# Keeping the written order in the feed-forward blocks of a two-layer trunk, and adding the residual inside PSUM

## The chip, the cores and the metric

The kernel runs on one core of one Trainium2 chip. The core has four engines that matter here: TensorE (PE in the profile; its weight loads are listed apart as PEld), VectorE (DVE), ScalarE (ACT) and GpSimd (POOL). A fifth, SyncE (SP), issues almost all transfers. The metric is the time on the device in microseconds, as the median of the runs shown. All arithmetic is meant to agree with a float32 reference.

## The reference, cut to what matters

Two layers; each has a token mixer (a gated recurrence with cross-attention into 256 memory tokens beside it) and a feed-forward part. The change lies in the feed-forward part:

```python
SEQ, D_MODEL, D_FF = 256, 2048, 5632
hn = _rmsnorm(h, norm_ffn[layer])
gate, up = jnp.split(hn @ w_gate_up[layer], 2, axis=-1)      # w_gate_up: 2048 x 11264
h = h + (jax.nn.silu(gate) * up) @ w_down[layer]             # w_down: 5632 x 2048
```

## The kernel before, in words

**Products.** The kernel multiplies float32 numbers by splitting each into a high part, rounded to the type fp32r, and a low part that holds the rest. A product is then three matmuls: high by high, high by low, low by high (L333, L334, L335 in the gate and up products; L249, L250, L251 in the down products). The tokens' factor is split once; the weights are split as they come. A weight tile is loaded in float32 into a buffer `raw` of 128 x 4 x 512 numbers (four of these buffers), by `new_raw`. `split` then lets ScalarE write the high part (a CAST, L207) and VectorE the low one (a subtraction, L208) into a tile `parts`, of which there are six; a tile holds two rows of 512. So each weight passes through SP's queue, ScalarE, VectorE and TensorE in turn.

**The feed-forward part.** The 5632 hidden columns are handled in eleven blocks of 512, b0 to b10 (`ffn`, `up_block`). A block takes the 2048 rows of the weights in eight pairs of 128 rows, and computes for the two halves of the tokens both gate and up: per pair a 2 x 2 by 2 x 2 product of tiles. `project_halves` does this in one of three ways, by the letter of the pair in the table `KINDS`. Letter S (Strassen's scheme, in Winograd's form) takes seven products, 21 matmuls; its sums of weight tiles are three more operations on VectorE (L350 on 1024 columns, L351 and L352 on 512), and the tiles are split in four pieces named `parts<number>a` to `d`: a of 512 columns, b, c, d of 1024. Letter O takes eight products, 24 matmuls, without sums, in pieces a and b. Letter H also takes eight products and 24 matmuls, with one sum of 512 columns and a third piece of 512. The seven partial results of the block, p1 to p7, lie in seven of the eight PSUM banks. From block 3 on, all blocks have the letters SSOSSOSS.

After the last pair of a block the seven results are added up into `s` and `e` (one COPY on ScalarE, L830; seven additions on VectorE, L833), the gate goes through SiLU (L835, ScalarE) and is multiplied by up (L836, VectorE). The product `s` is transposed on TensorE and split again (`make_quad`, L148 and L149), as the tokens' factor of the down product.

**The down products.** The down product sums over the eleven blocks in six parts (`PARTS`: block 0; blocks 1 and 2; 3 and 4; ... 9 and 10), each for four column groups of 512: `down(i, n)`. Two of these are done after each of the blocks b1 to b10, and the four of the last part at the end. A down product of two blocks is 48 matmuls in two banks, and `add_h` (L414, VectorE) then adds each bank of 128 x 512 to the residual `h`, which stays in SBUF.

**What sets the order.** The instructions are written in this order, but the framework's scheduler decides which goes first on each engine, within what buffers and data allow. Pieces of work such as the transposes are handed to a list (`later`) and let out between steps (`step`).

## Time and profile before

| what | value |
|---|---|
| median of 3 runs | 2323.36 us (2322.37 to 2323.85) |
| the profiled execution's own time | 2322.12 us |
| its span on the core | 2320.3 us |
| mean granted TensorE clock | 0.998 |
| matmul instructions (PE) | 11034, busy 2297.6 us (99% of the span) |
| weight loads (PEld) | 11034, busy 1934.7 us (83%) |
| VectorE | 2262 instructions, busy 1887.7 us (81%) |
| ScalarE | 1643 instructions, busy 1261.2 us (54%) |
| bytes moved by transfers | 435.51 MB, mean 188 GB/s |

The span is from the first to the last record on the core; the execution's own time is 1.8 us longer. A PE matmul's record lasts longer than the distance to the next one, because matmuls are pipelined; so PE is called busy nearly throughout, also where it waits for short times, and its waits are better read from the starts of its rows. By the starts of its instructions the span falls into: the memory tokens' product (5 to 105 us), the first mixer (105 to 447) with its output product (447 to 541), the first feed-forward part (541 to 1250), the second mixer with its output product (1250 to 1610), and the second feed-forward part (1610 to 2320). In the first feed-forward part block 8 begins at 1008.57 us, block 9 at 1071.72 and block 10 at 1134.89.

In the views, "f_p" are the gate and up results, "fd" the down results, "hf" the tokens' factor of the gate and up products, "s_8" the gated product of a block and its split halves, "tp_" a transposed tile in PSUM, "parts" the split weights. Single pieces keep their numbers: parts172 to parts179 are the eight pairs of block 8, and parts184 to parts191 those of block 9 in the first layer. The names are shared between the kernel before and the kernel after.

### The profile page before, as it was taken

The page shows a single profiled execution, that of the slowest core. Times are in us where ns is not written, and L with a number is a line of the kernel's source. Part 1 is how long each engine was busy: PE and PEld are TensorE (multiplying, and loading weights), DVE is VectorE, ACT ScalarE, POOL GpSimd, SP SyncE. Part 2 cuts the span into 40 slices and gives each one's busy share as a digit, 9 for nine tenths or more (in the row PEclk, how much of TensorE's full clock was granted, in tenths as well). Part 3 has the DMA queues.
Part 4 walks back from the last instruction along what each step waited for, and adds up shares of the span by engine and source line. Part 5 has one row for each costly group of instructions (what it writes and reads, how often), then busy time and mean ns, then how long its engine had stood idle before and what let it go on. Part 6 is the DMA issues. An engine that isn't in the chain of part 4 may idle for free.

```text
span 2320.3 us, 28901 instructions
## 1 busy us (share of the span) xinstructions
PE 2297.6 (99%) x11034; PEld 1934.7 (83%) x11034; DVE 1887.7 (81%) x2262; ACT 1261.2 (54%) x1643; POOL 22.2 (1%) x39
## 2 busy tenths in 40 slices
PE   9999999999999999999999999999999999999998
PEld 7888888888887888888889999988887888888886
DVE  5566565668999999999985665567999999999995
ACT  7543534455555555555555654455555555555563
POOL 0000000000000000000000000000000000000000
PEclk9999999999999999999999999999999999999999
DMA  8554545455556556566565445555555556656563
GB/s 316 192 172 162 164 150 176 145 182 176 186 188 212 200 188 205 189 209 208 183 226 167 150 150 167 161 199 164 178 203 198 201 187 210 202 189 210 200 217 127
DMA packets 229211, 435.51 MB, mean 188 GB/s; under 512 B 10028, under 2 KB 38992, under 8 KB 228816
## 3 DMA queue, kind: packets, MB, share of 16 engines
q1 hardware_dynamic: 227776, 429.40, 55.5%
q10 hardware_dynamic: 1296, 4.26, 0.5%
q8 instruction: 86, 1.41, 0.2%
q14 instruction: 53, 0.43, 0.1%
HBM read 430.48 MB, written 3.15 MB: 187 GB/s over the span
## 4 chain that ended last, share of the span: by engine, by line
PE 63%; DVE 25%; issue 6%; ACT 4%; DMA 0%; ACTq 0%; DVEq 0%; POOLq 0%; SPq 0%
PE f_p L334 5%; PE f_p L335 5%; PE f_p L333 4%; DVE raw L350 4%; DVE parts L208 4%; PE fd L250 3%; PE fd L249 3%; PE fd L251 3%; PE wo L251 3%; PE wo L249 3%; PE wo L250 3%; DVE raw L351 2%; DVE raw L352 2%; PE hgate L249 1%; PE gv L249 1%
## 5 line engine op out<-in xcount | busy, mean ns | idle before, releaser
L208 DVE TENSOR_TENSOR parts<-raw,parts 128x1024 fp32r<-128x1024 f32 (+3 forms) x490 | 557.7, 1147 | 289.1 <-ACT parts L207 288.2
L207 ACT CAST parts<-raw 128x1024 fp32r<-128x1024 f32 (+3 forms) x490 | 476.8, 991 | 424.6 <-PE wo L251 64.4
L350 DVE TENSOR_TENSOR raw<-raw 128x1024 f32<-128x1024 f32 x118 | 143.6, 1217 | 0.2
L351 DVE TENSOR_TENSOR raw<-raw 128x512 f32<-128x512 f32 x118 | 81.6, 692 | 3.9
L352 DVE TENSOR_TENSOR raw<-raw 128x512 f32<-128x512 f32 x118 | 81.6, 692 | 3.8
L414 DVE TENSOR_TENSOR h<-fd,h 128x512 f32<-128x512 f32 x94 | 61.9, 684 | 6.2 <-PE fd L251 6.1
L833 DVE TENSOR_TENSOR e<-f_p,e 128x512 f32<-128x512 f32 x66 | 44.9, 680 | 0.0
L835 ACT ACTIVATE s<-s,rf_r 128x512 f32<-128x512 f32 x44 | 31.8, 722 | 6.9 <-DVE s L833 6.9
L836 DVE SCALAR_TENSOR_TENSOR s<-e,rf_r,s 128x512 f32<-128x512 f32 x44 | 32.3, 742 | 0.0
L562 DVE COPY_PREDICATED sch<-mask,slh 96x512 f32<-96x512 uint8 (+3 forms) x15 | 10.8, 721 | 25.1 <-PE slh L578 25.1
L833 DVE TENSOR_TENSOR s<-f_p,e 128x512 f32<-128x512 f32 x44 | 29.5, 682 | 0.0
L578 PEld LDWEIGHTS slh<-Q,K 128*96 128x96 f32 (+3 forms) x240 | 25.4, 176 | 1.4
L249 PE MATMUL wo<-parts,y_3h 128*128 128x512 f32 x64 | 25.9, 405 | 0.0
L249 PE MATMUL wo<-parts,y_0h 128*128 128x512 f32 x64 | 25.7, 402 | 0.0
L250 PE MATMUL fd<-parts,s_3h 128*128 128x512 f32 x64 | 25.4, 396 | 0.0
L249 PE MATMUL fd<-parts,s_0h 128*128 128x512 f32 x64 | 25.3, 396 | 0.0
L249 PE MATMUL fd<-parts,s_2h 128*128 128x512 f32 x64 | 25.3, 396 | 0.0
L249 PE MATMUL fd<-parts,s_6h 128*128 128x512 f32 x64 | 25.3, 396 | 0.0
L249 PE MATMUL fd<-parts,s_4h 128*128 128x512 f32 x64 | 25.3, 396 | 0.0
L250 PE MATMUL fd<-parts,s_5h 128*128 128x512 f32 x64 | 25.3, 396 | 0.0
L249 PE MATMUL fd<-parts,s_8h 128*128 128x512 f32 x64 | 25.3, 396 | 0.0
L250 PE MATMUL fd<-parts,s_0h 128*128 128x512 f32 x64 | 25.3, 396 | 0.0
(5486 smaller groups left out, 7396.4 us busy)
## 6 DMA issues: line engine op xcount, KB each, us to landing
raw<-in_w_gate_up_dram SPq DMA_DIRECT2D x352, 512.0 KB, 4.0
raw<-in_w_down_dram SPq DMA_DIRECT2D x88, 1024.0 KB, 5.0
raw<-in_hgrn_w_in_dram SPq DMA_DIRECT2D x52, 1024.0 KB, 5.0
raw<-in_gla_w_in_dram SPq DMA_DIRECT2D x48, 768.0 KB, 4.3
raw<-in_w_out_dram SPq DMA_DIRECT2D x32, 1024.0 KB, 4.9
raw<-in_w_mem_kv_dram SPq DMA_DIRECT2D x15, 1024.0 KB, 8.2
raw<-in_gla_w_in_dram SPq DMA_DIRECT2D x8, 528.0 KB, 3.7
mtok<-in_mem_dram SPq DMA_DIRECT2D x4, 512.0 KB
```

The source lines that it names most:

```text
L207: nc.scalar.copy(out=both[:, 0, k:j, 0:m], in_=src[:, k:j, :])
L208: nc.vector.tensor_tensor(out=both[:, 1, k:j, 0:m], in0=src[:, k:j, :], in1=both[:, 0, k:j, 0:m].bitcast(F32), op=ALU.subtract)
L249: nc.tensor.matmul(acc, xh, hi[:, o:o + m], start=first, stop=False)
L250: nc.tensor.matmul(acc, xh, lo[:, o:o + m], start=False, stop=False)
L251: nc.tensor.matmul(acc, xl, hi[:, o:o + m], start=False, stop=last)
L333: nc.tensor.matmul(ps[b], xh, hi, start=first, stop=False)
L334: nc.tensor.matmul(ps[b], xh, lo, start=False, stop=False)
L335: nc.tensor.matmul(ps[b], xl, hi, start=False, stop=left[b] == 0)
L350: tt(out=raw[:, 0:2, :], in0=raw[:, 0:4:2, :], in1=raw[:, 1:2, :].broadcast_to([P, 2, 512]), op=ALU.subtract)
L351: tt(out=raw[:, 2, :], in0=raw[:, 2, :], in1=raw[:, 0, :], op=ALU.add)
L352: tt(out=raw[:, 3, :], in0=raw[:, 3, :], in1=raw[:, 2, :], op=ALU.subtract)
L833: nc.vector.tensor_tensor(out=out, in0=ps[p], in1=q, op=ALU.add)
```

## The change

Five things change, all of them in the feed-forward part except the smaller number of buffers and the form of the transposes, which also hold elsewhere.

1. **Order.** TensorE, VectorE and ScalarE are wrapped. While `Engine.kept` is set, each instruction that goes through the wrapper is to keep its written place on its engine. It is set from pair 3 of block 0 on, and cleared before the last four down products. All wrapped instructions carry the line of the wrapper.
2. **An agenda.** Inside the kept stretch the sums, the gate, the transposes, the splitting of `s`, and the writing back of `h` are queued with a key by `due` and let out by `mark`, which is called at each pair and at each half of a down product. The keys are 100 times the block plus a number: 0 to 7 for its pairs, 10 and 11 for the two halves of its first down product, 12 and 13 for its second. The table `WHEN` gives them for blocks 0, 1, 2, and 3 and later.
3. **Buffers.** There are three `raw` buffers and not four. Tiles that hold one row only (piece a of S, piece c of H) get a tag of their own, `part`, of half the size, with two buffers; the six `parts` remain.
4. **The residual.** In the down products of the first five parts ScalarE copies `h` into the two PSUM banks before the first matmul (`onto`), all matmuls accumulate onto it, and ScalarE copies the banks back into `h` (`give_back`). VectorE's `add_h` remains for the last part and for the mixers' output products.
5. **Letters.** Block 1 begins with H in place of S, and block 3 has H in place of S for its seventh pair; six more matmuls in each layer, 12 in all.

A transposed tile is also formed as one accumulation group of four transposes, where each had been its own instruction with its own start.

```diff
+    class Engine:
+        kept = False
+        def __init__(self, engine):
+            self.engine = engine
+        def __getattr__(self, name):
+            func = getattr(self.engine, name)
+            def issue(*args, **kwargs):
+                ins = func(*args, **kwargs)
+                if Engine.kept:
+                    tc.keep_in_program_order(ins)
+                return ins
+            return issue
...
+    pe, ve, ac = Engine(nc.tensor), Engine(nc.vector), Engine(nc.scalar)
+    waiting = []
+    def due(key, work):
+        waiting.append((key, len(waiting), work))
+        waiting.sort(key=lambda w: w[0])
+    def mark(key):
+        while waiting and waiting[0][0] <= key:
+            waiting.pop(0)[2]()
...
+    def turns(ps, srcs):
+        for i, src in enumerate(srcs):
+            pe.matmul(ps[:, i * P:(i + 1) * P], src, ident, start=i == 0, stop=i == len(srcs) - 1,
+                             is_transpose=True, skip_group_check=True)
...
-        return i, wts.tile([P, 4, 512], F32, tag="raw", name=f"raw{i}", bufs=4)
+        return i, wts.tile([P, 4, 512], F32, tag="raw", name=f"raw{i}", bufs=3)
 
     def split(src, name, by=2):
 
         n, m = src.shape[1:]
-        both = wts.tile([P, 2, 2, 512], F32R, tag="parts", name=f"parts{name}", bufs=6)
+        if n == 1:
+            both = wts.tile([P, 2, 1, 512], F32R, tag="part", name=f"parts{name}", bufs=2)
+        else:
+            both = wts.tile([P, 2, 2, 512], F32R, tag="parts", name=f"parts{name}", bufs=6)
...
+                    if key is not None:
+                        mark(key + qi)
+                    if onto and qi == 0:
+                        for t in range(NT):
+                            ac.copy(out=ps[0][t], in_=onto(t))
                 for k, (hi, lo) in enumerate(got[qi]):
-                    if k == 2 or (k == 0 and qi > 0):
+                    if key is None and (k == 2 or (k == 0 and qi > 0)):
                         step()
-                    first = qi == 0 and k == 0
+                    first = qi == 0 and k == 0 and not onto
...
+            Engine.kept = keep <= p
...
                 b11, b10 = split(raw[:, 2:4, :], f"{i}b")
+                mark(key + p)
...
-    KINDS = ("SHOSHOSO", "SHOSSOSO", "SHOSSOSO", "SSOSSOSS")
+    KINDS = ("SHOSHOSO", "HHOSSOSO", "SHOSSOSO", "SSOSSOHS", "SSOSSOSS")
+    WHEN = (dict(sums=101, gate=101, turn=((102, 103), (104, 105)), back=(13, 101)),
+            dict(sums=10, gate=12, turn=((12, 100), (12, 100)), back=(100, 101)),
+            dict(sums=10, gate=12, turn=((12, 101), (12, 101)), back=(100, 101)),
+            dict(sums=10, gate=11, turn=((13, 101), (13, 101)), back=(13, 101)))
...
-            ps = project_halves(forms, KINDS[min(b, 3)], w_gate_up[l], 512 * b, DFF + 512 * b, f"f{l}_{b}_")
-            e = work.tile([P, NT, 512], F32, tag="stg", name=f"e{l}_{b}", bufs=2)
...
-            for t, up in enumerate((e1, e0)):
-                nc.scalar.activation(out=s[:, t, :], in_=s[:, t, :], func=AF.Silu, scale=r[:, t:t + 1])
-                nc.vector.scalar_tensor_tensor(out=s[:, t, :], in0=up, scalar=r[:, t:t + 1], in1=s[:, t, :],
-                                               op0=ALU.mult, op1=ALU.mult)
...
+            ps = project_halves(forms, KINDS[min(b, 4)], w_gate_up[l], 512 * b, DFF + 512 * b, f"f{l}_{b}_",
+                                100 * b, 0 if b else 3)
+            when = WHEN[min(b, 3)]
+            def sums():
+                got["e"] = e = work.tile([P, NT, 512], F32, tag="stg", name=f"e{l}_{b}", bufs=2)
...
+                ac.copy(out=e0, in_=ps[1])
+                for out, p, q in ((s0, 2, e0), (e1, 6, e0), (s1, 7, e1), (e1, 5, e1), (e0, 5, s1),
+                                  (s1, 4, s1), (e1, 3, e1)):
+                    ve.tensor_tensor(out=out, in0=ps[p], in1=q, op=ALU.add)
...
+            def gate():
+                e, s = got["e"], got["s"]
+                for t in range(NT):
+                    ac.activation(out=s[:, t, :], in_=s[:, t, :], func=AF.Silu, scale=r[:, t:t + 1])
+                for t in range(NT):
+                    ve.scalar_tensor_tensor(out=s[:, t, :], in0=e[:, 1 - t, :], scalar=r[:, t:t + 1], in1=s[:, t, :],
+                                            op0=ALU.mult, op1=ALU.mult)
...
+            due(100 * b + when["sums"], sums)
+            due(100 * b + when["gate"], gate)
+            for j, (k0, k1) in enumerate(when["turn"]):
+                due(100 * b + k0, lambda j=j: turn(j))
+                due(100 * b + k1, lambda j=j: sq[b].put(2 * j, 2, got[j]))
...
-            ps = project(sq, PARTS[i], w_down[l], 512 * n, 512, f"fd{l}_{i}_{n}")
-            add_h(ps, 512 * n, 512)
+            hs = h[:, :, 512 * n:512 * n + 512]
+            ps = project(sq, PARTS[i], w_down[l], 512 * n, 512, f"fd{l}_{i}_{n}", onto=lambda t: hs[:, t, :], key=key)
+            def give_back():
+                for t in range(NT):
+                    ac.copy(out=hs[:, t, :], in_=ps[t])
+            due(back, give_back)
...
+                    down(*todo.pop(0), 100 * b + 10 + 2 * j, 100 * b + WHEN[min(b, 3)]["back"][j])
+        mark(100 * (DFF // 512 + 1))
+        Engine.kept = False
+        for n in range(NQ):
+            down(len(PARTS) - 1, n, None, None)
```

In the other hunks `nc.tensor`, `nc.vector` and `nc.scalar` become `pe`, `ve` and `ac`, and `project_halves` gets `key` and `keep` handed to it.

**VectorE between the down products of block 8 and the start of block 9.** `parts_0` and `parts_2` are the two halves of a down weight, `parts184a` to `d` the first pair of block 9, `fd_3_2_0` the first down product of block 8. Before:

```order
L208 TENSOR_TENSOR parts_2_7884<-raw_7879,parts_2_7884 128x1024
L836 SCALAR_TENSOR_TENSOR s_8_7816<-e_8_7815,rf_r,s_8_7816 128x512
L208 TENSOR_TENSOR parts_0_7917<-raw_7915,parts_0_7917 128x1024
L208 TENSOR_TENSOR parts_2_7920<-raw_7915,parts_2_7920 128x1024
L149 TENSOR_TENSOR s_8l<-tp_s_8h_7853,s_8h 128x512
L149 TENSOR_TENSOR s_8l<-tp_s_8h_7860,s_8h 128x512
L414 TENSOR_TENSOR h<-fd_3_2_0_0_7829,h 128x512
L414 TENSOR_TENSOR h<-fd_3_2_0_1_7830,h 128x512
L208 TENSOR_TENSOR parts_0_7949<-raw_7947,parts_0_7949 128x1024
L208 TENSOR_TENSOR parts_2_7952<-raw_7947,parts_2_7952 128x1024
L208 TENSOR_TENSOR parts184a<-raw_7981,parts184a 128x512
L208 TENSOR_TENSOR parts184b<-raw_7981,parts184b 128x1024
```

After:

```order
L137 TENSOR_TENSOR parts_0_7925<-raw_7923,parts_0_7925 128x1024
L137 TENSOR_TENSOR parts_2_7928<-raw_7923,parts_2_7928 128x1024
L137 TENSOR_TENSOR parts_0_7959<-raw_7957,parts_0_7959 128x1024
L137 TENSOR_TENSOR parts_2_7962<-raw_7957,parts_2_7962 128x1024
L137 TENSOR_TENSOR parts184a<-raw_8003,parts184a 128x512
L137 TENSOR_TENSOR parts184b<-raw_8003,parts184b 128x1024
L137 TENSOR_TENSOR raw_8003<-raw_8003 128x1024
L137 TENSOR_TENSOR raw_8003<-raw_8003 128x512 x2
L137 TENSOR_TENSOR parts184c<-raw_8003,parts184c 128x1024
L137 TENSOR_TENSOR parts184d<-raw_8003,parts184d 128x1024
```

The two additions onto `h` are gone from this place, and the two subtractions that split `s` (L149, `s_8l`) have moved from ahead of the last down weights to behind the first two pieces of the second pair (they are the rows after those shown).

**ScalarE at the same place.** `s_8h` is the high half of the transposed `s`, which waits for the transposes on TensorE. Before:

```order
L207 CAST parts_0_7949<-raw_7947 128x1024
L207 CAST parts_2_7952<-raw_7947 128x1024
L835 ACTIVATE s_8_7816<-s_8_7816,rf_r 128x512
L207 CAST parts184a<-raw_7981 128x512
L148 ACTIVATE s_8h<-tp_s_8h_7853 128x512
L148 ACTIVATE s_8h<-tp_s_8h_7860 128x512
L207 CAST parts184b<-raw_7981 128x1024
L207 CAST parts184c<-raw_7981 128x1024
L207 CAST parts184d<-raw_7981 128x1024
```

After:

```order
L137 CAST parts_0_7959<-raw_7957 128x1024
L137 CAST parts_2_7962<-raw_7957 128x1024
L137 COPY h<-fd_3_2_0_0_7839 128x512
L137 COPY h<-fd_3_2_0_1_7840 128x512
L137 CAST parts184a<-raw_8003 128x512
L137 CAST parts184b<-raw_8003 128x1024
L137 CAST parts184c<-raw_8003 128x1024
L137 CAST parts184d<-raw_8003 128x1024
L137 CAST parts185a<-raw_8049 128x512
L137 CAST parts185b<-raw_8049 128x1024
L137 ACTIVATE s_8h<-tp_s_8h_7967 128x512
L137 ACTIVATE s_8h<-tp_s_8h_7972 128x512
```

The rows `COPY h<-fd` are the write-back; it stands between the last down weight and the first piece of block 9. The splits of `s` have moved from behind `parts184a` to behind `parts185b`. By the keys of `WHEN` for block 3 and later (`back=(13, 101)`), the first down product of a block is written back at the second half of the second one, and the second at pair 1 of the next block, where its copies stand behind the last row shown, ahead of `parts185c`.

**VectorE at the end of block 8's last pair.** `f_8_p` are the seven results of the block, `parts_0_7833` (after: `7843`) is the first half of the first down weight. Before:

```order
L833 TENSOR_TENSOR s_8_7816<-f_8_p_7534,e_8_7815 128x512
L208 TENSOR_TENSOR parts179d<-raw_7776,parts179d 128x1024
L208 TENSOR_TENSOR parts_0_7833<-raw_7831,parts_0_7833 128x1024
L833 TENSOR_TENSOR e_8_7815<-f_8_p_7546,e_8_7815 128x512
L208 TENSOR_TENSOR parts_2_7836<-raw_7831,parts_2_7836 128x1024
L833 TENSOR_TENSOR s_8_7816<-f_8_p_7542,e_8_7815 128x512
L208 TENSOR_TENSOR parts_0_7881<-raw_7879,parts_0_7881 128x1024
L833 TENSOR_TENSOR e_8_7815<-f_8_p_7538,e_8_7815 128x512
L833 TENSOR_TENSOR e_8_7815<-f_8_p_7538,s_8_7816 128x512
L833 TENSOR_TENSOR e_8_7815<-f_8_p_7530,e_8_7815 128x512
L833 TENSOR_TENSOR s_8_7816<-f_8_p_7550,s_8_7816 128x512
```

After:

```order
L137 TENSOR_TENSOR parts179d<-raw_7800,parts179d 128x1024
L137 TENSOR_TENSOR parts_0_7843<-raw_7841,parts_0_7843 128x1024
L137 TENSOR_TENSOR parts_2_7846<-raw_7841,parts_2_7846 128x1024
L137 TENSOR_TENSOR s_8_7850<-f_8_p_7552,e_8_7849 128x512
L137 TENSOR_TENSOR e_8_7849<-f_8_p_7564,e_8_7849 128x512
L137 TENSOR_TENSOR s_8_7850<-f_8_p_7560,e_8_7849 128x512
L137 TENSOR_TENSOR e_8_7849<-f_8_p_7556,e_8_7849 128x512
L137 TENSOR_TENSOR e_8_7849<-f_8_p_7556,s_8_7850 128x512
L137 TENSOR_TENSOR s_8_7850<-f_8_p_7568,s_8_7850 128x512
L137 TENSOR_TENSOR e_8_7849<-f_8_p_7548,e_8_7849 128x512
L137 TENSOR_TENSOR parts_0_7887<-raw_7885,parts_0_7887 128x1024
```

Before, the seven additions stand between low parts of weights, over eleven rows, the first of them ahead of `parts179d`; after, they are seven rows in one piece behind the first down weight.

More of the change, by code (lines that the diff above doesn't have):

```diff
@@ L248, in project @@
                             acc = ps[i][t][:, 0:m]
-                            nc.tensor.matmul(acc, xh, hi[:, o:o + m], start=first, stop=False)
-                            nc.tensor.matmul(acc, xh, lo[:, o:o + m], start=False, stop=False)
-                            nc.tensor.matmul(acc, xl, hi[:, o:o + m], start=False, stop=last)
+                            free = dict(skip_group_check=True) if onto else {}
+                            pe.matmul(acc, xh, hi[:, o:o + m], start=first, stop=False, **free)
+                            pe.matmul(acc, xh, lo[:, o:o + m], start=False, stop=False, **free)
+                            pe.matmul(acc, xl, hi[:, o:o + m], start=False, stop=last, **free)
             if by_tile is not None:
```

188 lines of the change are left out of this document (91 added, 97 removed).

## The prediction

> **What bounds the kernel now.** I read the page first, then the windows that hold one stage each, then the chain and the timeline of one block.
>
> ```profile
> PE 2297.6 (99%) x11034; PEld 1934.7 (83%) x11034; DVE 1887.7 (81%) x2262; ACT 1261.2 (54%) x1643; POOL 22.2 (1%) x39
> ...
> DVE  5566565668999999999985665567999999999995
> ...
> DMA  8554545455556556566565445555555556656563
> ...
> PE 63%; DVE 25%; issue 6%; ACT 4%; DMA 0%; ACTq 0%; DVEq 0%; POOLq 0%; SPq 0%
> ```
>
> TensorE is called busy 99% of the time, and the whole-span average seems to close the case. But VectorE's digits stand at 9 from slice 11 to 20 and again from slice 30 on: the two feed-forward parts. There two engines are full together, and the chain gives VectorE a quarter of the span. Which of them ends last has to be read inside a block.
>
> ```profile
> core 0: us, PE busy (x) PEld busy (x) DVE busy (x) ACT busy (x) POOL busy (x), PEclk, DMA share, GB/s
> 104.55:126.31 21.76, 21.76 (x97) 18.02 (x96) 10.94 (x9) 10.58 (x12) 0.00 (x0) 1.00 0.76 268
> 690.79:731.93 41.14, 39.70 (x171) 31.53 (x170) 40.56 (x44) 23.92 (x29) 0.00 (x0) 1.00 0.54 179
> 1008.57:1047.99 39.42, 39.19 (x171) 31.68 (x170) 38.83 (x42) 23.19 (x27) 0.00 (x0) 1.00 0.56 187
> 1008.57:1071.72 63.15, 62.92 (x279) 51.16 (x278) 62.44 (x70) 36.08 (x41) 0.00 (x0) 1.00 0.60 200
> ```
>
> The first row is a stretch of the first mixer in which TensorE runs unhindered: 96 distances of 512-column matmuls in 21.76 us, 0.2267 us each, at clock 1.00. With it the other rows become tests. The gate and up products of block 8 (third row, from the first of them to the first down matmul) hold 170 distances: 170 x 0.2267 = 38.54 us. They took 39.42, so TensorE waited 0.88 us. The same count in block 3 (second row) took 41.14: it waited 2.60 us. The whole of block 8 (last row) takes 63.15 us, with VectorE busy for 62.44 of them: a **steady block is set by VectorE**, and TensorE would need 63.15 - 0.88 = 62.27 us at most. These steady blocks are b4 to b10, with the same letters and two full down products, seven in each layer.
>
> ```profile
> 1016.12 0.79 DVE parts174a L208
> ...
> 1018.40 0.69 DVE parts175a L208
> ...
> 1025.14 0.68 DVE parts176a L208
> ...
> 1059.90 1.18 DVE s_8l L149 x2
> ...
> 1061.62 0.68 DVE h L414
> ...
> 1062.30 2.27 DVE parts L208 x2
> 1064.56 0.60 DVE parts184a L208
> ```
>
> This is the chain through the same block, start and length of each piece. It never leaves VectorE for long. A pair O costs VectorE 1018.40 - 1016.12 = 2.28 us, a pair S 1025.14 - 1018.40 = 6.74. One split of 1024 columns costs 1.135 (half of 2.27), one operation of 512 columns 0.60, a split of `s` 0.59 (half of 1.18).
>
> ```profile
> 606.76 0.61 PE L333 MATMUL f_p<-parts96c,hf_4h 128*128 128x512 f32 x2
> 608.05 0.50 PE L333 MATMUL f_p<-parts96d,hf_4h 128*128 128x512 f32 x1 [0.68 <-ACT parts96d L207]
> ...
> 697.59 0.63 PE L333 MATMUL f_p<-parts113c,hf_1h 128*128 128x512 f32 x2
> 698.93 0.51 PE L333 MATMUL f_p<-parts113d,hf_1h 128*128 128x512 f32 x1 [0.71 <-ACT parts113d L207]
> ...
> 713.58 0.61 PE L333 MATMUL f_p<-parts116c,hf_4h 128*128 128x512 f32 x2
> 714.69 0.50 PE L333 MATMUL f_p<-parts116d,hf_4h 128*128 128x512 f32 x1 [0.49 <-ACT parts116d L207]
> ...
> 1045.88 0.40 PE L335 MATMUL f_p<-parts179b,hf_7l 128*128 128x512 f32 x1
> 1046.50 0.51 PE L333 MATMUL f_p<-parts179d,hf_7h 128*128 128x512 f32 x1 [0.23 <-ACT parts179d L207]
> ```
>
> Here TensorE's waits are seen, each for piece d of a pair S, which comes last out of VectorE's sums. In block 1 (parts96d) two matmuls and the wait took 1.29 us for 0.45: 0.84 lost. In block 3 (parts113d, parts116d) 0.89 and 0.66 are lost. In block 8 only the last pair loses: 0.62 for 0.23 before parts179d.
>
> **The change part by part.**
>
> *The residual moved off VectorE.* A block has two down products of two banks, so four additions (L414) leave VectorE: 4 x 0.60 = 2.40 us. VectorE's need falls to 63.15 - 2.40 = 60.75, below TensorE's 62.27. If nothing else came up, a block would then cost what TensorE needs, 62.2 in round numbers.
>
> *What ScalarE gets for it.* Eight copies of 512 columns, four into PSUM and four out. No row of before writes a float32 copy into PSUM; the nearest is the copy out of PSUM:
>
> ```profile
> L830 ACT COPY e<-f_p x22: 568/576/582, 574.3 to 2240.4; 128x512 f32<-128x512 f32 x22
> ...
> 1050.76 2.00 ACT L207 CAST parts<-raw 128x1024 fp32r<-128x1024 f32 x2
> 1053.62 2.11 ACT L207 CAST parts<-raw 128x1024 fp32r<-128x1024 f32 x2 [0.86 <-DMA raw<-in_w_down_dram]
> ...
> 1057.67 0.62 ACT L207 CAST parts184a<-raw 128x512 fp32r<-128x512 f32 x1 [1.32 <-PE fd L251]
> 1058.88 1.09 ACT L148 ACTIVATE s_8h<-tp_s_8h 128x512 fp32r<-128x512 f32 x2 [0.59 <-PE tp_s_8h L160]
> 1061.04 1.05 ACT L207 CAST parts184b<-raw 128x1024 fp32r<-128x1024 f32 x1 [1.07 <-PE fd L251]
> ```
>
> Between 0.50 (two 1024-column casts last 2.00, a quarter of it) and 0.62 us (a 512-column cast) I take 0.576 each, and for a pair the 1.09 of the two at 1058.88: 4.4 us on an engine that is busy 36.08 of 63.15. Time as such is hidden. Place is not. In the listing the copies back of the first down product stand ahead of the cast `parts184a`, which begins the next block, and they wait for that product's last matmul. Behind them on ScalarE are all casts of the next block, and behind those VectorE and TensorE. So there is now a **ring**, from the first down matmul of one block to that of the next: 48 matmuls (48 x 0.2267 = 10.88), a hand-over to ScalarE (0.25, taken from the 0.23 that TensorE sat idle before parts179d), two copies back (1.09), the cast of piece a (0.62), the gap until VectorE's piece b has its cast (half of 2.00 for a 1024-column cast against VectorE's 0.60 for piece a: 0.40), VectorE's eight pairs with the two splits of `s` that now lie among them (6 x 6.74 + 2 x 2.28 + 1.18 = 46.18), and the last 14 matmuls of the block after the last piece d (14 x 0.2267 = 3.17). Sum: 62.59. That is above TensorE's 62.2 and below 63.15. It gains 0.56 a block, 14 x 0.56 = 7.8. Were the copies at either end of 0.50 and 0.62, the ring would move by 0.1 to 0.15, some 2 us in all.
>
> [...]
>
> *The other copies.* The copies of `h` into PSUM are issued when the first weights' casts and the copy `e` are done, and the first down matmul comes behind them on TensorE. They are needed when the block's products end, and ScalarE idles then (0.86 us before the cast at 1053.62). I take zero; uncovered, two copies would cost TensorE 1.15 a block. The second copies back stand ahead of the cast parts185c, when the second down product has ended; VectorE does its sums for the second pair meanwhile (2.5 us, the 6.74 of a pair S without its four splits), which covers them. Zero; uncovered, 1.15 as well.
>
> *Blocks 1 to 3.* VectorE loses one pair S to H in block 1 and in block 3: it does 6.74 us for S, and for H two 1024-column splits, a sum and a 512-column split, 2 x 1.135 + 2 x 0.60 = 3.47. It is thus 3.27 us earlier, and in block 3 also 2.4 from the residual. TensorE pays 3 matmuls each, 6 x 0.2267 = 1.36 per layer. Block 1's 0.84 goes. Of block 3's 2.60 I let 0.25 stand, since the waits lie in pairs 1, 4 and 7 and the new H is pair 6: the relief ahead of pair 1 comes from the residual alone. Per layer -0.84 - 2.35 + 1.36 = -1.83, twice -3.7.
>
> *Buffers.* The third `raw` buffer decides how early a transfer can be issued. Its rows:
>
> ```profile
> raw<-in_w_gate_up_dram SPq DMA_DIRECT2D x352, 512.0 KB, 4.0
> raw<-in_w_down_dram SPq DMA_DIRECT2D x88, 1024.0 KB, 5.0
> ...
> raw<-in_w_mem_kv_dram SPq DMA_DIRECT2D x15, 1024.0 KB, 8.2
> ```
>
> Count from the first down matmul. The cast of parts184a is due after 10.88 + 0.25 + 1.09, at 12.2 us. Its buffer is that of the second weight tile of the first down product. VectorE splits the last piece d 3.2 us before zero, then two halves (2.27), the seven sums (4.2) and two more halves (2.27): the buffer is free at 5.6 at the latest, and 4.0 us later, at 9.6, the tile is there; with both halves one behind the other, at 10.4. The cover is some 2 us: zero. A landing of 8.2 takes it away (a rival). At the start of the kernel the fourth tile now waits for the first buffer. The transfers are busiest there (8 tenths in the page's first slice), so an earlier issue would mostly wait in the queue: zero, and at most one landing of 8.2, once.
>
> *Order as such.* The same instructions stand in the kept order on TensorE but for the transposes, and the new order of VectorE puts the seven sums behind one down weight. They end some 4 us after zero, and the gate and the transposes that follow them are used one block's products later at the earliest. Zero; the bounds are TensorE's own 62.2 below, and above the 63.15 that stands now.
>
> The **sum**: -7.8 - 3.7 = -11.5 us. Against the profiled execution, 2322.12, that is 2310.6; its span, 1.8 shorter, would be 2308.8. The median of the runs shown lies 1.2 above the profiled execution, so 2311.9, rounded **2312**.
>
> **The rivals.**
>
> 1. *TensorE alone bounds.* If the ring has slack (shorter hand-overs, an earlier last piece), a steady block costs 62.2, a gain of 0.95: 2323.4 - 13.3 - 3.7 = 2306. For it: the ring exceeds TensorE's need by only 0.4 in a sum of seven terms. Against it: the copies back do stand ahead of the cast.
> [...]
> 2. *The waits only move.* The kept order leaves engines waiting where the scheduler had filled in, a steady block stays at 63.15, and only blocks 1 to 3 gain: 2319.7. For it: in the listing the sums stand in one piece, and the splits of `s` behind six other subtractions and the three sums of pair S. Against it: VectorE gets 2.4 us of room.
> 3. *Slower: the third buffer is late.* Should parts184's tile land 8.2 us after its release, it lands at 13.8, 1.6 after the cast is due. The ring becomes 62.59 + 1.6 = 64.2, 1.05 above 63.15 in fourteen blocks: +14.7 - 3.7, so 2334. The cast waits from a landing of 6.6 us on, and the kernel is slower than before from 7.4 on. For it: with four buffers there is already a wait of 0.86 for a down weight at 1053.62. Against it: medians of 4.0 and 5.0 and a transfer share of 0.60 in block 8.
> 4. *Nothing moves.* Gains in blocks 1 to 3 and losses by the new order cancel: 2323.
>
> **How the numbers follow.** The ring 0.48, TensorE alone 0.22, moved waits 0.13, the late buffer 0.10, nothing 0.07. The likeliest gives 2312. The range for 8 in 10 reaches from 2302, 4 below the first rival for what its terms leave open (14 blocks by 0.3), to 2321, above the second's 2319.7; the slower rival lies outside. 0.2% is 4.6 us, about what a measurement of this kernel can tell from no change. The ring and TensorE alone are faster by more than that (0.70), and some of the moved waits (0.05); the rest of these and the cancelled gains give 0.15 within; the late buffer 0.10 slower.
>
> **What would show it.** The steady block's period, from one block's first product to the next: 62.6 for the ring, 62.2 for TensorE, 63.15 for moved waits, above 64 for the buffer. VectorE busy about 60.0 in it (62.44 - 2.40). TensorE's wait before the last pair's piece d: still there but shorter in the ring, gone in the first rival. ScalarE idle ahead of `COPY h<-fd`, released by TensorE, and the cast `parts184a` right behind it. In the late-buffer case that cast is released by a transfer. The rows of parts96d, parts113d and parts116d without their waits. I am wrong if the period stays above 63, or if new waits of TensorE stand at the first down matmul for the copies into PSUM.

## The result, and the profile after

The changed kernel takes 2304.31 us (median of 4 runs, 2303.68 to 2304.86), the kernel before 2322.99 beside it. The ratio is 0.9919, with a 95% interval of 0.9902 to 0.9936. The forecast was 2312 with a range of 2302 to 2321. The time lies in the range, but it is nearer to the first rival's 2306 (TensorE alone) than to the forecast. The profiled execution took 2304.44 us, with a span of 2302.6.

The page of the changed kernel: the first line, VectorE's digits, and the chain's shares.

```profile
PE 2288.3 (99%) x11046; PEld 1943.1 (84%) x11046; DVE 1839.0 (80%) x2170; ACT 1335.9 (58%) x1799; POOL 22.3 (1%) x39
...
DVE  5566565668999999999975664557899999999995
...
PE 98%; DVE 1%; issue 0%; ACT 0%; DMA 0%; POOLq 0%; DVEq 0%; SPq 0%; ACTq 0%
```

VectorE's digits still stand at 9 in the feed-forward parts, although it has 49 us less to do. The line of shares has changed altogether: TensorE 98% where it was 63%, VectorE 1% where it was 25%. What a digit of 9 means is told by the chain, not by the digit.

The windows of the changed kernel, from one block's first product to the next: blocks 3, 4, 6 and 9 of the first layer.

```profile
core 0: us, PE busy (x) PEld busy (x) DVE busy (x) ACT busy (x) POOL busy (x), PEclk, DMA share, GB/s
691.24:754.09 62.85, 62.85 (x283) 51.94 (x281) 60.03 (x67) 39.93 (x51) 0.00 (x0) 1.00 0.62 209
754.09:816.65 62.56, 62.39 (x280) 51.43 (x278) 60.79 (x67) 40.09 (x50) 0.00 (x0) 1.00 0.59 203
878.92:941.18 62.26, 62.26 (x279) 51.42 (x278) 60.49 (x66) 40.08 (x50) 0.00 (x0) 1.00 0.59 202
1065.77:1128.04 62.27, 62.27 (x279) 51.43 (x278) 60.50 (x66) 40.09 (x50) 0.00 (x0) 1.00 0.59 202
```

A steady block takes 62.27 us (63.15 before). VectorE is busy for 60.5 of it, near the 60.0 expected. Block 3, with three matmuls more, takes 62.85 (64.86 before).

Where the 17.7 us between the two spans lie follows from the starts of the blocks in both traces. Blocks 0 to 3 give 2.65 in the first layer and 2.70 in the second. Everything from block 4 to the end of the down products gives 6.19 and 6.32. Against that stands 1.09 by which the first feed-forward part starts later (541.95 against 540.86), and 0.92 come from the end, where the last matmul is followed by 8.86 us and not by 9.78. Neither can be put down to the change. In the executions of the experiments below the first feed-forward part starts anywhere between 540.9 and 541.95 with either set of buffers. The end is 8.86 in all of them (to 0.02), also behind the old kernel with one part of the change; the instructions after the last matmul are the same before and after and start at the same distances, so the 0.92 lies behind the issue of the last transfers. There is one trace of the kernel before, and whether 9.78 is its usual end is open.

The chain of the changed kernel in block 8 has six pieces.

```profile
1002.99 0.68 PE fd L137 x3
1003.67 39.61 PE f_p L137 x174
1043.28 16.32 PE fd L137 x72
1059.60 0.87 PE tp_s_8h L137 x8
1060.47 5.46 PE fd L137 x24
1065.93 1.13 PE f_p L137 x5
```

TensorE follows upon TensorE. But a chain shows what ended last and not by how much. The timeline has the forecast's ring in it; the rows are given in the order ScalarE, VectorE, and TensorE at the end of the block's last pair:

```profile
1053.57 1.27 ACT L137 COPY h<-fd 128x512 f32<-128x512 f32 x2 [1.77 <-PE fd L137]
1054.73 0.62 ACT L137 CAST parts184a<-raw 128x512 fp32r<-128x512 f32 x1
...
1055.39 0.69 DVE L137 TENSOR_TENSOR parts184a<-raw,parts184a 128x512 fp32r<-128x512 f32 x1 [0.44 <-ACT parts184a L137]
...
1039.55 0.76 PE L137 MATMUL f_p<-parts179d,hf_7h 128*128 128x512 f32 x2
1040.14 0.39 PE L137 MATMUL f_p<-parts179d,hf_7l 128*128 128x512 f32 x1
```

ScalarE waits 1.77 us for the first down product, copies it back, casts, and VectorE has waited for that cast. At the other end of the ring two matmuls on piece d take 0.59 us to the next (1040.14 - 1039.55), where two distances of 0.2267 would be 0.45: TensorE still waits 0.14 us for VectorE. Ring and TensorE are thus almost equally long. Which of them sets 62.27 is what the first experiments ask.

### The profile page after: what moved, and what is told of

Its sections match the earlier page's. It is cut to its first block, busy times and chain, and to the rows that moved or that the text cites. A ratio compares the mean times of both kernels' runs of the same rounds, so it can differ in the third digit from the quotient of the medians.

```text
span 2302.6 us, 29032 instructions
## 1 busy us (share of the span) xinstructions
PE 2288.3 (99%) x11046; PEld 1943.1 (84%) x11046; DVE 1839.0 (80%) x2170; ACT 1335.9 (58%) x1799; POOL 22.3 (1%) x39
## 4 chain that ended last, share of the span: by engine, by line
PE 98%; DVE 1%; issue 0%; ACT 0%; DMA 0%; POOLq 0%; DVEq 0%; SPq 0%; ACTq 0%
PE f_p L137 37%; PE fd L137 21%; PE wo L137 8%; PE ggate L137 3%; PE gv L137 3%; PE hgate L137 3%; PE hv L137 3%; PE hf L137 3%; PE hq L137 3%; PE mk L137 2%; PE mv L137 2%; PE gk L137 1%; PE gq L137 1%; PE gx L137 1%; PE slh L137 1%; PE hx L137 1%
## 5 line engine op out<-in xcount | busy, mean ns | idle before, releaser
L137 ACT CAST parts<-raw 128x1024 fp32r<-128x1024 f32 (+3 forms) x490 | 477.2, 990 | 407.3 <-PE wo L137 63.8
L137 DVE TENSOR_TENSOR raw<-raw 128x1024 f32<-128x1024 f32 (+1 forms) x354 | 304.9, 861 | 7.9
L137 ACT COPY h<-fd 128x512 f32<-128x512 f32 x80 | 46.2, 588 | 53.4 <-PE fd L137 50.5
L137 ACT COPY fd<-h 128x512 f32<-128x512 f32 x80 | 44.0, 582 | 0.0
L137 PE MATMUL wo<-parts,y_3h 128*128 128x512 f32 x128 | 40.5, 398 | 0.0
L137 PE MATMUL fd<-parts,s_9h 128*128 128x512 f32 x128 | 39.7, 391 | 0.0
L137 PE MATMUL wo<-parts,y_1h 128*128 128x512 f32 x128 | 39.4, 389 | 0.0
L137 PE MATMUL wo<-parts,y_2h 128*128 128x512 f32 x128 | 39.4, 389 | 0.0
L137 PE MATMUL fd<-parts,s_10h 128*128 128x512 f32 x128 | 39.4, 389 | 0.0
L137 PE MATMUL fd<-parts,s_1h 128*128 128x512 f32 x128 | 39.4, 389 | 0.0
L137 PE MATMUL fd<-parts,s_7h 128*128 128x512 f32 x128 | 39.4, 389 | 0.0
```

Of the source, the lines that this page charges most:

```text
L137: ins = func(*args, **kwargs)
```

## The experiments

All ran beside the kernel before, three rounds each. "Period" is the time from one steady block's first product to the next, read from each trace.

**1. Order free.** The scheduler orders, all else stays.

```diff
-            Engine.kept = keep <= p
+            Engine.kept = False
```

> The changed kernel with Engine.kept never set: the scheduler orders again; the residual in PSUM, the agenda, the buffers and the letters stay. Theory R (the relief of VectorE by 2.4 us a block is what counts, whoever orders): a steady block takes 62.2 to 62.5 us against 62.27 now, time 2304 to 2308. Theory K (the written order is what counts): the scheduler puts the copies back or the sums where they hold up the next block, a steady block takes 62.9 or more, time above 2312.

Measured 2308.65 us (ratio 0.9938, 0.9923 to 0.9953), periods of 62.1 to 62.5 with single blocks of 63.0 to 63.3. The down products of block 1 move past later work; blocks 1 to 3 take 170.8 us together where the kept order takes 169.7. So the written order is worth 4.3 us of the 18.7. This is 0.7 above theory R's window and 3.4 below theory K's. The runs that follow show that it does not stay this simple.

**2. The additions back on VectorE, order kept.**

```diff
-            ps = project(..., onto=lambda t: hs[:, t, :], key=key)
+            ps = project(..., key=key)
             def give_back():
-                for t in range(NT):
-                    ac.copy(out=hs[:, t, :], in_=ps[t])
+                add_h(ps, 512 * n, 512)
```

> The changed kernel, order kept, but the residual is added by VectorE again, four additions of 512 columns a block at the places where the copies back stood; no copies into PSUM. Theory R: VectorE is full again (8 pairs 45.0, splits of s 1.2, sums 4.2, gate 1.3, down splits 9.1, additions 2.4, together 63.2 us), a steady block takes 63.1 to 63.3 and the time is 2316 to 2319. Theory K (order counts): below 62.6 a block, time at most 2308.

Measured 2330.93 us (1.0035, 1.0022 to 1.0048): slower than the kernel before. The direction is theory R's, but the period is 63.77 and not 63.2. VectorE is busy for 62.69 of it, and the timeline of this run shows what the sum of durations had left out:

```profile
1051.86 0.68 DVE L137 TENSOR_TENSOR s<-f_p,e 128x512 f32<-128x512 f32 x1
1052.45 0.68 DVE L137 TENSOR_TENSOR e<-f_p,e 128x512 f32<-128x512 f32 x1
1053.24 0.69 DVE L137 TENSOR_TENSOR s<-f_p,e 128x512 f32<-128x512 f32 x1
1054.04 0.69 DVE L137 TENSOR_TENSOR e<-f_p,e 128x512 f32<-128x512 f32 x1
1054.64 0.68 DVE L137 TENSOR_TENSOR e<-f_p,s 128x512 f32<-128x512 f32 x1
1055.43 0.69 DVE L137 TENSOR_TENSOR s<-f_p,s 128x512 f32<-128x512 f32 x1
```

An addition starts 0.60 us after the one ahead, but 0.79 after one whose result it reads or whose operand it overwrites (second to third, third to fourth, fifth to sixth). Three such places in a block are 0.57 us, and 63.2 + 0.57 = 63.77. These three are also the longest stretches (0.10 each) in which VectorE idles in this block, so VectorE sets it. The order that writes the seven sums in one piece costs this on VectorE, and it can only pay where VectorE has room.

**3. The old letters, order kept.**

```diff
-    KINDS = ("SHOSHOSO", "HHOSSOSO", "SHOSSOSO", "SSOSSOHS", "SSOSSOSS")
+    KINDS = ("SHOSHOSO", "SHOSSOSO", "SHOSSOSO", "SSOSSOSS", "SSOSSOSS")
```

> The changed kernel with the letters of before (blocks 1 and 3 with S where it has H): 12 matmuls less, 2.7 us of TensorE. Theory R: block 1's wait of 0.95 comes back in each layer, since no relief lies ahead of it, and block 3's is partly taken up by the relief of the residual, 0 to 1.2 in each layer: time 2303.5 to 2306, no clear difference from 2304.3. Rival (the letters carry the gain of blocks 1 to 3): both waits come back whole, 0.95 + 2.5 a layer less 1.36, time 2308 to 2309.

Measured 2307.59 us (0.9934, 0.9919 to 0.9949), between the two. Neither theory has it right, since the letters act apart. Block 1 takes 53.57 us with S against 54.25 with H: the 0.68 of three matmuls, and no wait. Its H buys nothing. Block 3 takes 64.87 against 62.85, in spite of three matmuls fewer: its waits are back, now all in the last pair, as the timeline of this run shows.

```profile
726.42 0.39 PE L137 MATMUL f_p<-parts119b,hf_7l 128*128 128x512 f32 x1
728.22 0.49 PE L137 MATMUL f_p<-parts119d,hf_7h 128*128 128x512 f32 x1 [1.41 <-ACT parts119d L137]
729.48 0.50 PE L137 MATMUL f_p<-parts119d,hf_7h 128*128 128x512 f32 x1 [0.77 <-DVE parts119d L137]
```

Here 1.80 and 1.26 us pass for 0.23 each: 2.6 lost. VectorE's debt from the S pairs is carried forward to block 3's end, and the H of block 3 pays it there.

**4. Three more copies in the ring.** ScalarE copies the same bank three times more, between the copies back and the next block's first cast.

```diff
                     ac.copy(out=hs[:, t, :], in_=ps[t])
+                for _ in range(3 if back % 100 == 13 and back > 400 else 0):
+                    ac.copy(out=hs[:, 1, :], in_=ps[1])
```

> The changed kernel with three more copies of 512 columns (each about 0.53 us) on ScalarE behind the write-back of a block's first down product and ahead of the first cast of the next block, in blocks 4 to 10 (the same bank copied again). ScalarE has 25 us to spare in a block. Ring theory: the ring has 0.26 us of slack below TensorE's 62.27, so a block grows by 1.59 - 0.26 = 1.33 where a next block follows, 12 times: +16, time 2320. TensorE theory (no ring near): 0, time 2304 to 2305.

Measured 2327.02 us (1.0016, 1.0006 to 1.0025). The period is 64.07 (blocks of 64.05 and 64.09, one of 65.95).

```profile
1060.46 3.12 ACT L137 COPY h<-fd 128x512 f32<-128x512 f32 x5 [1.77 <-PE fd L137]
1063.47 0.62 ACT L137 CAST parts184a<-raw 128x512 fp32r<-128x512 f32 x1
```

From the first copy to the cast there are 3.01 us, where the changed kernel has 1.16 (1054.73 - 1053.57): 1.85 more. The period grows by 1.80. So the ring exists, ScalarE's 22 idle microseconds in a block do not help, and its slack is 0.05 us. The ring theory had the mechanism but not the size: it expected 2320, with copies of 0.53 and a slack of 0.26. The pure TensorE theory is rejected: in the changed kernel the ring is all but exactly as long as the block.

**5. The ring shortened.** The copies back of the first down product go behind the casts of the next block's pieces a and b.

```diff
-            dict(sums=10, gate=11, turn=((13, 101), (13, 101)), back=(13, 101)))
+            dict(sums=10, gate=11, turn=((13, 101), (13, 101)), back=(100, 101)))
```

> The changed kernel with the copies back of a block's first down product placed behind the casts of pieces a and b of the next block, in blocks 3 to 10 (back = (100, 101) in place of (13, 101)). Ring theory, with the slack that the run with three more copies left (below 0.1): the ring of 62.27 now loses its two copies, 1.16, and falls to 61.1 or so, and TensorE alone sets a block, 62.27 less the 0.17 by which its matmuls still wait: 62.10. 12 to 14 blocks by 0.17: -2.0 to -2.4, time 2302. Rival (TensorE's own need is 62.27): no difference, 2304. Rival (the transfer into the third buffer is next): the cast is released by a transfer and the block stays at 62.2 to 62.3.

Measured 2300.81 us (0.9904, 0.9888 to 0.9921). The window of block 8, and ScalarE ahead of block 9, in this run:

```profile
1001.87:1063.97 62.10, 62.10 (x280) 51.51 (x279) 61.03 (x67) 40.00 (x50) 0.00 (x0) 1.00 0.62 208
...
1050.72 0.62 ACT L137 CAST parts184a<-raw 128x512 fp32r<-128x512 f32 x1 [0.98 <-DMA raw<-in_w_gate_up_dram]
1052.07 1.05 ACT L137 CAST parts184b<-raw 128x1024 fp32r<-128x1024 f32 x1 [0.73 <-DMA raw<-in_w_gate_up_dram]
1053.03 1.06 ACT L137 COPY h<-fd 128x512 f32<-128x512 f32 x2
```

The period is 62.09 in all steady blocks of both layers, to 0.01, and TensorE's matmuls follow each other without a wait: this is TensorE's own need. The count agrees: 174 gate and up matmuls and 96 down matmuls at 0.2267, and 0.87 for eight transposes, are 62.08. The changed kernel's 62.27 was the ring's, by 0.18. Of the 3.5 us gained on the change some 0.6 are not the edit's, since this execution's first feed-forward part starts at 541.35 and not at 541.95. With the copies out of the way the cast waits for the transfer into the third raw buffer (0.98), as the buffer rival foresaw, but with TensorE as the bound this costs nothing.

**6. The fourth corner: order free, additions on VectorE.** Experiments 1 and 2 in one kernel.

> The fourth corner of a square: order free (as in the free run at 2308.7) and the residual added by VectorE (as in the run at 2330.9); agenda, buffers and letters of the change. Theory I (the kept order costs where VectorE is full and pays only where it is relieved): the scheduler packs VectorE as before, a steady block takes 63.15 to 63.3 and the time is 2319 to 2323, some 9 below the kept order with the same work. Rival (letters, buffers or the agenda made the 2330.9): 2328 or more here too.

Measured 2346.60 us (1.0099, 1.0084 to 1.0114), the rival's side: theory I is wrong. The periods are 63.8 to 66.0, most of them near 65. The waits of this run in block 8:

```profile
ACT parts L137 <- DMA raw<-in_w_down_dram: 4.6, 2, 2.8
ACT parts175a L137 <- DMA raw<-in_w_gate_up_dram: 4.1, 1, 4.1
ACT parts185a L137 <- DMA raw<-in_w_gate_up_dram: 3.2, 1, 3.2
ACT parts178a L137 <- DMA raw<-in_w_gate_up_dram: 3.2, 1, 3.2
ACT parts176a L137 <- DMA raw<-in_w_gate_up_dram: 2.3, 1, 2.3
ACT parts179a L137 <- DMA raw<-in_w_gate_up_dram: 2.3, 1, 2.3
```

The casts wait for transfers in most pairs, 19.7 us in all. With three raw buffers a tile's transfer has to wait until VectorE has finished with the tile three back: in block 8 of the changed kernel every listed wait of SP's queue ends with a low part on VectorE, the longest, 7.0 us, with that of parts173d. That VectorE comes to these parts later in this run, where it has the additions to do as well, was not shown. In the kernel before only one wait of 0.9 us for a transfer stands in such a block.

**7 and 8. The old buffers, order free.** Four raw buffers, all tiles in the six `parts`, once with the additions on VectorE and once with the residual in PSUM.

```diff
-... tag="raw", name=f"raw{i}", bufs=3)
+... tag="raw", name=f"raw{i}", bufs=4)
-        if n == 1:
-            both = wts.tile([P, 2, 1, 512], F32R, tag="part", name=f"parts{name}", bufs=2)
-        else:
-            both = wts.tile([P, 2, 2, 512], F32R, tag="parts", name=f"parts{name}", bufs=6)
+        both = wts.tile([P, 2, 2, 512], F32R, tag="parts", name=f"parts{name}", bufs=6)
```

> The free run with the additions on VectorE (2346.6, about 65.2 us a block) with the buffers of before: four raw, six parts, no tag for one-row tiles. In that run ScalarE's casts waited some 20 us a block for transfers. Buffer theory: with the fourth raw buffer these waits go, a block takes 63.15 to 63.3 and the time is 2319 to 2323. Rival (the agenda's order of writing is what the scheduler handles badly): 2335 or more.

> The free run (2308.7: order free, residual in PSUM, agenda and letters of the change) with the buffers of before. Buffer theory: the blocks that took 63 there fall to 62.2 and the time is 2305 to 2307, so that of the 4.3 us between free and kept order most is the third buffer. Order theory: no better than 2308, the 4.3 us are the order's.

With the additions on VectorE: 2330.88 us (1.0036, 1.0022 to 1.0049), 15.7 faster than with the new buffers but 8 slower than the kernel before; between the two theories. The waits for transfers fall from 19.7 to 0.6 us in block 8, so some of the loss was the buffers'. The period is still 64.0. What differs from the kernel before is now the agenda, the letters and the form of the transposes; these three were not taken apart. With the residual in PSUM: 2320.63 us (0.9992, 0.9982 to 1.0001), 12 us *slower* than with the new buffers. The buffer theory is wrong, and the order theory gave no price for a loss of this size. The window of its block 8, and pieces of the chain: the start of block 8, then from the end of VectorE's work on it to the next block:

```profile
1009.26:1072.41 63.15, 62.92 (x280) 51.20 (x278) 60.05 (x66) 40.06 (x50) 0.00 (x0) 1.00 0.59 200
...
1009.50 1.06 ACT parts173b L137
...
1045.71 1.23 DVE parts179c L137
1046.94 0.04 issue
1046.98 2.93 PE f_p L137 x11
1049.91 16.33 PE fd L137 x72
1066.24 0.87 PE tp_s_8h L137 x8
1067.11 5.47 PE fd L137 x24
...
1072.65 1.06 ACT parts185b L137
```

VectorE has 2.4 us less to do than before (60.05 busy, not 62.44), and the period is 63.15 all the same, the very number of the kernel before. The chain names the loop: the cast of parts185b waits for the *end of the second down product*, VectorE then works from 185b to the last pair, TensorE takes the last products, the down products, and their end releases the next such cast: 1072.65 - 1009.50 = 63.15. What joins them is a `parts` tile. There are six, handed out in turn, and a down weight takes two of them, the second down product of a block therefore four. Then come 184a, b, c, d, 185a and 185b: when piece a takes a whole tile as well, 185b is the sixth after the last down tile and must have that one, the last half of the second down product. With a tag of its own for piece a, 185b is the fourth, and its tile is the one that the first weight of that product held in its second half.

The additions to `h` lay outside this loop. The kernel before shows the same cast, released by nothing that the profile names, right behind the last down matmul, and VectorE turning to its piece b soon after:

```profile
1071.49 0.39 PE L251 MATMUL fd<-parts,s_6l 128*128 128x512 f32 x1
1071.96 1.06 ACT L207 CAST parts185b<-raw 128x1024 fp32r<-128x1024 f32 x1 [1.40 <-issue]
1073.13 1.22 DVE L208 TENSOR_TENSOR parts185b<-raw,parts185b 128x1024 fp32r<-128x1024 f32 x1
```

The cast starts 0.47 us after the last down matmul. So it does behind blocks 5 to 9 of the first layer, in the kernel before and in experiments 7, 8 and 9, all with the old buffers. In the changed kernel the same cast starts 3.8 us *ahead* of that matmul. The loop is thus there in the kernel before. But there VectorE has not waited for the cast: it is busy with the additions to `h` and with piece a until then, and begins piece b 0.11 us after the cast has ended, where in experiment 8, waiting, it begins 0.03 after. So VectorE set the kernel before, with the loop some 0.08 us behind it (an estimate from these two distances).

**9. The old buffers, order kept.** The edit of 7 and 8 on the changed kernel.

> The changed kernel with the buffers of before: four raw, and the one-row tiles in the six parts. Theory: the 1.09 us by which the first mixer starts later with three buffers comes back (first gate and up product at 540.9 and not 541.95), and the feed-forward blocks lose if a small piece holds a whole parts tile: between 0 and 0.7 a block; time 2303 to 2313. Rival (three buffers hold up the steady blocks): a block below 62.2, time below 2302.

Measured 2381.20 us (1.0249, 1.0234 to 1.0264), far outside both. The period is 67.9. The waits of this run in block 8 include these two:

```profile
ACT parts173b L137 <- PE fd L137: 2.1, 1, 2.1
...
ACT parts185a L137 <- PE fd L137: 2.0, 1, 2.0
```

Here the profile names the down product as what the second pair's casts wait for. In kept order the rest of ScalarE's queue, the splits of `s` and the second copies back, stands behind the waiting cast. So the half-size tiles are not an economy of memory on the side: the kept order cannot do without them. Some 19 us of the 77 lost against the change come from TensorE's clock, as the last section works out. Whether it is the tag alone, with the number of raw buffers indifferent, was not tried apart; the chain of experiment 8 speaks for the tag, and with the fourth raw buffer the waits for transfers were shorter (0.6 us in block 8 of experiment 7 against 19.7 in experiment 6).

**10. The residual alone, in the kernel before.** `onto` and the copies back in the old code, scheduler, old buffers, old letters, old transposes.

```diff
+                    if onto and qi == 0:
+                        for t in range(NT):
+                            nc.scalar.copy(out=ps[0][t], in_=onto(t))
...
-            add_h(ps, 512 * n, 512)
+            for t in range(NT):
+                nc.scalar.copy(out=hs[:, t, :], in_=ps[t])
```

> The kernel before with one part of the change alone: h is copied into PSUM ahead of each down product of the first five parts and copied back by ScalarE, order by the scheduler, old buffers, old letters, no agenda. Theory R (the relief of VectorE is the larger part): a steady block falls from 63.15 to 62.1 to 62.5, blocks 1 and 3 keep most of their waits: time 2308 to 2312. Rival (relief needs the order): a steady block above 62.9, time above 2318.

Measured 2327.88 us (1.0023, 1.0014 to 1.0032): slower than before, with VectorE busy for 60.16 of a period of 63.65. Theory R falls: with the old buffers this relief of VectorE is worth less than nothing. Two rows show why:

```profile
1073.99 1.27 ACT L862 COPY h<-fd 128x512 f32<-128x512 f32 x2 [1.43 <-PE fd L255]
...
1076.23 1.23 DVE L208 TENSOR_TENSOR parts185b<-raw,parts185b 128x1024 fp32r<-128x1024 f32 x1 [1.69 <-ACT parts185b L207]
```

The copies back of the second down product stand ahead of the cast in the loop, which now starts 0.96 us after the last down matmul and not 0.47, and VectorE stands waiting for it. The 0.49 more are the 0.50 by which the period grows.

This kernel keeps the old transposes, and part of `h` is presumably left out of its sums, which come out wrong; the instructions that are timed are all there. Why they do was not shown, and no run here tried the form of the transposes apart.

**11. Letters of blocks 0 and 1.**

```diff
-    KINDS = ("SHOSHOSO", "HHOSSOSO", "SHOSSOSO", "SSOSSOHS", "SSOSSOSS")
+    KINDS = ("SHOSSOSO", "SHOSSOSO", "SHOSSOSO", "SSOSSOHS", "SSOSSOSS")
```

> The changed kernel with H back to S in block 1 (pair 0) and H to S in block 0 (pair 4); block 3 keeps its H. 12 matmuls less, 2.72 us of TensorE; VectorE has 37.45 busy of 42.47 in block 0. Theory: block 1's H covers no wait (with the old letters block 1 had none in kept order, its period was 53.6), the debt shows at block 3's end, and one H there pays it: the whole 2.7 is gained, time 2301.6. Rival (the debt of two S more is carried on to block 3): a wait of 1 to 3 before the last pieces of block 3 in each layer, time 2304 to 2308.

Measured 2302.90 us (0.9913, 0.9898 to 0.9927). Block 0 takes 41.79 where it took 42.47, as worked out; block 1 takes 54.7 where S alone had given 53.57. The debt of block 0's S is presented in block 1 already (1.0 us before piece c of its fifth pair), not in block 3. Half of the theory holds.

**12. The best of these.** The copies back later (5), block 1 with its old letters (3), block 3 with its H.

```diff
+    KINDS = ("SHOSHOSO", "SHOSSOSO", "SHOSSOSO", "SSOSSOHS", "SSOSSOSS")
...
+            dict(sums=10, gate=11, turn=((13, 101), (13, 101)), back=(100, 101)))
```

> The changed kernel with the copies back of the first down product behind the casts of the next block's first pieces (2300.8 alone) and block 1 with its old letters, block 3 with its H. Theory: 3 matmuls less in each layer, 0.68, and no new wait in block 1 (period 53.57, as in the run with the old letters); block 3 pays with its H: 2300.8 - 1.4 = 2299.4. Rival (block 1's S leaves a debt that block 3's one H does not pay): a wait in block 3, 2301 to 2303.

Measured 2299.28 us (2299.23 to 2299.69), ratio to the kernel before 0.9900 (0.9885 to 0.9914): the 2299.4 expected, and 5.0 us below the change. Block 1 takes 53.57, block 3 62.8, a steady block 62.09.

## Why the prediction was right or wrong

*What bounds the kernel.* "A steady block is set by VectorE" was right, but only by some 0.08 us: right behind VectorE's own work lay the loop through the `parts` tiles. Experiments 8 and 10 relieve VectorE and find the loop at 63.15 and 63.65; experiments 2 and 6 open the loop and find VectorE (63.77) or the third raw buffer (65). The row that I passed over was ScalarE's 1.40 before parts185b, released by "issue".

*The residual.* "VectorE's need falls below TensorE's 62.27": right as a sum (60.5 busy, 60.0 forecast). What should follow, that the block falls with it, failed on its own (experiments 8 and 10). It follows only together with the buffers that I had costed at zero. To that extent the forecast came out by luck: the tag for the half-size tiles removed a bound that it had not seen.

*The ring.* Right in kind (experiment 4), mis-sized: 62.59 forecast, 62.27 measured. The term is the first: "48 matmuls (10.88), a hand-over (0.25)". The copies back start 10.46 us after the first down matmul (1053.57, where that matmul starts at 1043.11, and the matmuls of the first bank end before those of the second), not after 11.13. The copies and the cast take a little longer than their terms, and VectorE begins piece a at 12.28 where the sum had 12.84. What follows took 49.99 where the sum had 49.75. The steady blocks so gained 0.88 and not 0.56 each, 12.5 us in all against 7.8. That a copy which waits on ScalarE holds up the casts listed behind it was assumed; experiment 4 shows it here, where three more copies put off the cast of parts184a by 1.85 us and lengthen the block by 1.80.

*TensorE's need.* 62.2 assumed, 62.09 measured in experiment 5, and the count of matmuls shown there could have been made from the trace before. The weight loads of the trace before give an estimate as well: they are busy for 18.02 of 21.76 us in the unhindered stage, 82.8%, and for 51.16 us in block 8, and 51.16/0.828 = 61.8, a room of 1.4 us a block where 1.06 was there. At the floor the share is 51.51 of 62.10, 82.9%, which agrees with the 82.8% of the unhindered stage; the estimate was low because block 8 before showed 51.16 us of loads and a block at the floor shows 51.51.

*Blocks 1 to 3.* -1.83 a layer forecast, -2.65 and -2.70 measured. The H of block 3 works as described (experiment 3); block 1's 0.84 would have gone without an H (experiments 3 and 12), so that 0.68 of the 1.36 for the matmuls is paid for nothing. Of the 0.8 that the sum missed, 0.3 lie in block 2, for which it had no term.

*The buffers.* Zero was wrong. The new set of buffers is worth 12 us with the scheduler (2308.65 against 2320.63) and 77 in kept order (2304.31 against 2381.20), which is put down to the tag for half-size tiles, by argument and not by a run of its own. Three raw buffers in place of four cost when VectorE has the additions to do (waits for transfers of 19.7 us against 0.6 in block 8, experiments 6 and 7); that they cost nothing here is argued from the waits. The slower rival was the right mechanism with its point not reached: the transfer is next in line once the copies are out of the way (0.98 in experiment 5).

*Order as such.* Zero forecast; 4.3 us faster with relief and tag (2304.31 against 2308.65). With the additions on VectorE it is 15.7 faster than the free order with the same buffers, but slower than the kernel before. The form of the transposes changes nothing in time: they follow each other at 0.109 us before and after.

*The chances.* The ring (0.48) has the mechanism that set the changed kernel's block, TensorE alone (0.22) came nearer in time, because the two differ by 0.18 us a block and not by 0.4. The pieces of the change do not add up one by one: the residual alone loses 5 us (2327.88), order, buffers and letters without it lose 8 (2330.93), and all together gain 18.7.

## What to carry to other kernels

An engine that is busy 99% of a stage may be its bound and still be worth nothing to relieve (VectorE, 62.44 of 63.15 us before, and periods of 63.15 and 63.65 with it relieved in experiments 8 and 10): look for a loop through a buffer pool that has nearly the same length, by asking of each wait with no named releaser which tile it waits for and who held that tile last. Before trusting a relief, take the relief alone and see whether the period moves; here it did not fall until the tiles had room. When a copy has to stand in a queue whose order is kept, put it behind the first work of the next stage and not ahead of it: the same copies cost 0.18 us a block in one place and nothing in the other.

## What the runs showed of the hardware

Two things were not expected. These additions of 512 columns on VectorE follow each other at 0.60 us, but at 0.79 when one uses what the one ahead wrote or overwrites what it read (rows of experiment 2). And in experiment 9 TensorE ran at half its clock for some stretches, with a mean granted clock of 0.990 where the other runs have 0.998 or 0.999. There two matmuls of block 8's last pair come late, 1.80 and 1.26 us after the ones ahead of them, and then seven distances are 0.427 us and not 0.227, with a granted clock of 0.50. The windows of that run:

```profile
1061.00:1066.00 5.00, 3.24 (x14) 2.11 (x12) 4.88 (x6) 3.01 (x4) 0.00 (x0) 1.00 0.55 203
1067.69:1070.68 2.99, 2.99 (x9) 2.30 (x7) 2.82 (x4) 2.99 (x5) 0.00 (x0) 0.50 0.87 322
1071.00:1076.00 5.00, 5.00 (x23) 4.10 (x23) 4.89 (x7) 3.18 (x6) 0.00 (x0) 0.99 0.53 193
```

The trace's record of the granted clock holds twelve such stretches in the two feed-forward parts, each 3.41 us long. In the first layer they start at 794.58, 862.85, 931.11, 999.38, 1067.64 and 1200.76. Block 9 of that layer has the same two waits (1.81 and 1.26) and no such stretch; it takes 66.33 us, and blocks 5 to 8, each with one, take 67.9. Twelve times that difference is 19 us, an estimate of what the clock adds to experiment 9. In experiment 3 the same waits (1.80 and 1.26) are not followed by it at all, and in experiment 4 it appears once, in the block of 65.95 us. So the waits alone do not decide it; what does, these runs do not show.
